# Two-layer streaming attention encoder: the probabilities of both heads turned by DMA transposes in the second layer

## The chip, the cores and the metric

The kernel runs on one core of one Trainium2 chip. The metric is the time of one execution on the device in microseconds; before the change the median of three runs is 2216.19 us (2215.74 to 2218.65).

## The reference

Two attention layers over a prompt of 2048 frames and a sample of 64 frames, model width 1024, 16 heads of 64. The change lies in the second layer's prompt attention. Cut to that:

```python
def gated_attention_layer(x_p, x_s, ck, cv, norm_g, w_in, q_g, k_g, w_out, ...):
    qp, kp, vp, gp = project(x_p, norm_g, w_in, q_g, k_g, n_heads, n_kv)   # RMS norm, one matmul, norms of q and k
    op = prompt_band_attention(qp, kp, vp, past_chunks, bias_fn, sinks)     # own chunk of 64 and 8 before it
    y_p = x_p + (op * jax.nn.silu(gp)) @ w_out
    ...

# inside, for each head and chunk (second layer: no sinks)
s = q @ k.T * dh ** -0.5 + bias
p = jax.nn.softmax(s, axis=-1)
o = p @ v
```

Inputs and outputs are float32. The kernel keeps that precision with half-precision matmuls by splitting most operands into a high part and a remainder (hi = f16(x), lo = x - hi) and adding their products.

## The kernel before, in words

The first layer (`layer_a`), its output projection, the second layer (`layer_b`) and its output projection follow each other. The order of TensorE's instructions is written out by hand: attention steps alternate with pieces of projection matmuls, the "filler". `filler.to(mark)` emits projection work up to a mark. The other engines and the DMA queue of SP are ordered by a scheduler, within the dependencies and within hints: `bg.anchor(...)` names instructions behind which later background work (the norms of queries and keys, gates, splits of weights and activations) has to stand on the same engine. Each engine runs its instructions in order.

The second layer runs over 8 head pairs, `hp` 0 to 7, and in each over 9 units: 8 of 256 prompt frames (two tiles of 128) and the sample. A unit of the prompt has four attention steps, in the order tile 0 and tile 1 of head 0, then tile 0 and tile 1 of head 1. A step (`scores(it, i, h)`) is:

- TensorE: scores of 128 queries against up to 640 keys into an `sb` buffer of PSUM (L1416, L1417). There are two `sb` buffers.
- VectorE: adds the bias and takes the minimum of the negated scores (L1420) into `p` (float32) and `nm`.
- ScalarE: exp and the sums (L1429).

The products with the values need the probabilities with keys on the partitions, so each 128x128 block is transposed. `TURNED` (L54) lists the heads that do this by DMA; it holds for head pairs 1 to 7 only (`turned(it, h)`), not for head pair 0 and not for the sample.

- A head in `TURNED`: VectorE adds log(2^14) to `nm` ahead of exp (L1425). `parts` copies `p` to f16 on ScalarE (L1463) and subtracts that from `p` on GpSimd (L1464), both into one of three slots of a tile that the profile calls `values`. One step later `turn_p` issues the DMA transpose on SP (L1472) into a `pt` tile; there are two `pt` buffers, one for each head and unit. `turned_products` (matmuls at L1561) follows `LAG` = 4 steps after the step of the second tile.
- Another head: one step later `values` transposes block by block on TensorE (L844) into a new `sb` buffer; ScalarE (L816) and VectorE (L817) split that into `ph` and `pl`. `products` (matmuls at L1600) follows three steps after the step of the second tile.

When head 1 is done, the unit's gate is transposed into an `sb` buffer and multiplied in (L1237, L1247, L1249, L1250).

The queries and keys of a unit come from `head_norm`: squares on GpSimd (L756), sums on VectorE (L757), two GpSimd steps (L760 adds a constant, L761 takes the power -1/2), scaling on VectorE (L774), then TensorE transposes into `tp` and ScalarE and VectorE split them (L1355 to L1371). The copies `q<-q` go over SP (L1360), the projections' inputs too (`xx<-xsb`, L527).

Of the kernel before, what the change touches and what calls it, by code (L numbers as in the profile page):

```python
# [50 lines left out]
HB, WB_, PB, VB = 2.0 ** 10, 2.0 ** 14, 2.0 ** 14, 16.0  # L51
LAG = 4
HALF = 5 * 2 * P
TURNED = (0,)  # L54

@with_exitstack
def hybrid_encoder_kernel(
# [47 lines left out]
    def psum(tag, cols, bufs, pool=None):  # L105
        uid[0] += 1
        return (pool or pp).tile([P, cols], F32, tag=tag, name=f"{tag}_{uid[0]}", bufs=bufs)
# [77 lines left out]
    def times(dst, a, c):  # L185
        nc.vector.tensor_scalar(dst, a, c, 1.0, op0=ALU.mult, op1=ALU.mult)
# [33 lines left out]
    def input_across(h):  # L220
# [4 lines left out]
        times(o[:, 1:2], e, 1 / (HB * WB_))  # L225
        times(o[:, 2:3], e, 0.5 / VB if h > 0 and len(TURNED) == 2 else 0.5 / (VB * PB))

# [194 lines left out]
    bg = Background()  # L422
# [833 lines left out]
    def layer_b():  # L1256
# [126 lines left out]
        def scores(it, i, h):  # L1383
# [50 lines left out]
            if turned(it, h):  # L1434
                parts(it, i, h, p, nk // P)
            if c == w - 1:
                nc.vector.reciprocal(it.sm[:n, :w], it.sm[:n, :w])
                if turned(it, 0) and len(TURNED) == 1:
                    part = it.sm[:n, TURNED[0] : w : 2]
                    nc.vector.tensor_scalar(part, part, PB, 1.0, op0=ALU.mult, op1=ALU.mult)  # L1440
# [14 lines left out]
        def turned(it, h):  # L1455
            return it.unit[0] != NU and it.hp > 0 and h in TURNED

        def parts(it, i, h, p, m):
            held["turn"] = r = (held["turn"] + 1) % 3
            it.two = it.two if i else {}  # L1460
            it.two[i] = two = held["two"][:, 5 * r : 5 * r + m]
            pv = p.rearrange("p (c q) -> p c q", q=P)[:, :m]
            hi = nc.scalar.copy(two[:, :, 0, :], pv)  # L1463
            lo = nc.gpsimd.tensor_tensor(two[:, :, 1, :], pv, two[:, :, 0, :], op=ALU.subtract)  # L1464
            bg.anchor(hi, lo)
            it.two[i] = two.rearrange("p c l q -> p (c l q)")

        def turn_p(it, i, h, two):
# [32 lines left out]
        def then(it, i, h):  # L1501
            late = it.hp > 0 and len(TURNED)
            if it.unit[0] == NU:
                return [
                    (1, "values", (it, i, h)), (2 + late, "call", lambda: sample_outputs(it)),
                    (3 + late, "call", lambda: sample_turned(it)),
                ]
            last = i == len(it.unit[2]) - 1
            if turned(it, h):
                two = it.two[i]  # L1510
                todo = [(1, "call", lambda: turn_p(it, i, h, two))]
                return todo + [(LAG, "call", lambda: turned_products(it, h))] * last
            return [(1, "values", (it, i, h))] + [(2 + late, "products", (it, h))] * last
# [55 lines left out]
        def gates(it):  # L1569
            u, T, tiles = it.unit  # L1570
            n = tiles[0][2]
            GT = psum_b("sb", 1024, 2) if it.hp and len(TURNED) else psum("tp", 512, 1)
            for e, (_, t0, _) in enumerate(tiles):
# [348 lines left out]
```

## Time and profile before

| | |
|---|---|
| median of three runs | 2216.19 us |
| the profiled execution | 2214.94 us, span 2213.1 us |
| granted TensorE clock, mean | 0.991 |
| busy share of the span | PE 95%, DVE 71%, ACT 64%, POOL 45% |
| DMA transposes (L1472) | 112, from 1055.0 to 2048.1 us, median 3.5 us from issue to landing |

PE is TensorE's matmuls, PEld its weight loads, DVE VectorE, ACT ScalarE, POOL GpSimd, SP the engine that issues the DMAs. In rows of groups, "x112 | 140.0, 1250 | 243.5" means 112 instructions, 140.0 us busy in total, 1250 ns each on average, and 243.5 us of idle time of the engine just ahead of them, with what ended it. In rows of waits the three numbers are the total in us, how many, and the longest. In rows of the timeline they are the start and the duration in us.

### The profile page before, as it was taken

Reading aid. Unit: us, or ns where it says so; the run is one execution under the profiler, and the core shown is the slowest. Engines: PE = TensorE matmul, PEld = TensorE weight load, DVE = VectorE, ACT = ScalarE, POOL = GpSimd, SP = SyncE. Lnnn points to the kernel's source line nnn. Section 1 sums busy time; section 2 is a strip of 40 time slices with the busy share of each in tenths; the row PEclk is TensorE's granted clock in tenths of the full one; section 3 lists DMA queues with packets and bytes.
Section 4 is the critical chain, followed back from the end, with each engine's and each line's share of the span. In section 5 each row is a group of like instructions: output and inputs, shape, how many; then the busy total and the mean of one; then the engine's idle time right before and its main releaser. Section 6 shows DMA issues by size and latency. Waiting matters only on the chain. (4 is left out here: it accounts for less than half of the span.)

```text
span 2213.1 us, 41369 instructions
## 1 busy us (share of the span) xinstructions
PE 2102.7 (95%) x13441; PEld 1522.1 (69%) x13441; DVE 1563.9 (71%) x4105; ACT 1425.7 (64%) x3610; POOL 1004.9 (45%) x1509
## 2 busy tenths in 40 slices
PE   7999999999999999989999999999999998998999
PEld 6887888788889997556555555555555555556888
DVE  6769777677676456778676777877767778677642
ACT  6878878777785333666666766766667667576420
POOL 5645544334454455853444444444454445443000
PEclk9999999999999999999999999999999999999999
DMA  8856546856546667545465565654756546345664
GB/s 274 275 162 215 179 127 219 234 160 195 170 129 184 210 204 244 171 143 167 107 186 133 130 177 130 173 148 121 186 133 155 159 111 172 91 104 136 199 200 124
DMA packets 383096, 372.87 MB, mean 168 GB/s; under 512 B 174672, under 2 KB 320352, under 8 KB 382848
## 3 DMA queue, kind: packets, MB, share of 16 engines
q1 hardware_dynamic: 382880, 370.23, 58.0%
q8 instruction: 106, 1.74, 0.3%
q14 instruction: 110, 0.90, 0.1%
HBM read 257.59 MB, written 73.43 MB: 150 GB/s over the span
## 5 line engine op out<-in xcount | busy, mean ns | idle before, releaser
L679 PE MATMUL pj<-wh,xx 128*128 128x512 f16 (+2 forms) x1648 | 643.4, 390 | 5.8 <-ACT pb L702 4.1
L681 PE MATMUL pj<-wh,xx 128*128 128x512 f16 (+2 forms) x1648 | 625.5, 380 | 2.5 <-POOL xx L564 2.5
L680 PE MATMUL pj<-wh,xx 128*128 128x512 f16 x1024 | 391.5, 382 | 0.0
L1429 ACT ACTIVATE p<-p,nm 128x640 f32<-128x640 f32 (+5 forms) x264 | 198.9, 753 | 213.6 <-DVE nm L1420 108.0
L1765 PE MATMUL pj<-xx,wh 128*128 128x264 f32 (+1 forms) x1024 | 290.0, 283 | 8.5 <-DVE res L1775 4.1
L1766 PE MATMUL pj<-xx,wh 128*128 128x264 f32 (+1 forms) x1024 | 287.7, 281 | 0.0
L1464 POOL TENSOR_TENSOR values<-p,values 128x640 f16<-128x640 f32 (+2 forms) x112 | 140.0, 1250 | 243.5 <-ACT values L1463 243.5
L680 PE MATMUL pj<-wl,xx 128*128 128x512 f32 (+1 forms) x624 | 233.9, 375 | 2.2 <-DVE wl L470 2.2
L564 POOL TENSOR_TENSOR xx<-xraw,xx 128x528 fp32r<-128x528 f32 (+4 forms) x144 | 184.9, 1303 | 87.8 <-ACT xx L563 74.6
L1420 DVE CUSTOM_DVE_ANT_0 p<-sb,BT 128x640 f32<-128x640 f32 (+5 forms) x272 | 195.6, 719 | 38.3 <-PE sb L1417 35.6
L1250 POOL TENSOR_TENSOR o<-gt,o 128x256 f32<-128x256 f32 (+1 forms) x132 | 101.1, 766 | 206.2 <-ACT p L1156 89.6
L761 POOL TENSOR_TENSOR f<-f,mhalf 128x4 f32<-128x4 f32 (+2 forms) x187 | 187.0, 1000 | 13.8
L681 PEld LDWEIGHTS <-xx 128*128 128x128 f16 x1024 | 100.9, 99 | 125.9 <-issue 3.9
L774 DVE TENSOR_TENSOR pa<-pa,f 128x256 f32<-128x256 f32 (+3 forms) x221 | 136.5, 618 | 55.1 <-POOL f L761 50.6
L1156 ACT ACTIVATE p<-p,nm 128x257 f32<-128x257 f32 (+2 forms) x272 | 134.3, 497 | 50.1 <-DVE nm L1150 41.7
L756 POOL TENSOR_TENSOR sq<-pa 128x256 f32<-128x256 f32 (+2 forms) x187 | 123.7, 663 | 72.5 <-ACT pa L715 38.2
L679 PEld LDWEIGHTS <-xx 128*128 128x128 f16 x1024 | 101.0, 99 | 71.5 <-issue 2.7
L680 PEld LDWEIGHTS <-xx 128*128 128x128 f16 x1024 | 100.9, 99 | 70.3 <-issue 2.9
L817 DVE SCALAR_TENSOR_TENSOR pl<-sb,ph 128x640 f16<-128x640 f32 (+4 forms) x144 | 106.2, 737 | 58.2 <-ACT ph L816 56.5
L1767 PE MATMUL pj<-xx,wl 128*128 128x264 f32 x512 | 145.0, 283 | 1.0 <-DVE wl L463 1.0
L1767 PE MATMUL pj<-xx,wh 128*128 128x264 f16 x512 | 142.1, 277 | 1.3 <-DVE wh L460 1.3
L1150 DVE CUSTOM_DVE_ANT_0 p<-sa,BT,nsink 128x256 f32<-128x256 f32 (+2 forms) x272 | 117.3, 467 | 34.6 <-PE sa L844 29.5
(273 smaller groups left out, 5290.7 us busy)
## 6 DMA issues: line engine op xcount, KB each, us to landing
xx<-xsb SPq DMA_DIRECT2D x112, 512.0 KB, 4.2
xx<-xsa SPq DMA_DIRECT2D x88, 512.0 KB, 4.8
xraw<-oga SPq DMA_DIRECT2D x64, 264.0 KB, 3.6
xraw<-ogb SPq DMA_DIRECT2D x64, 264.0 KB, 3.6
xsa<-xx SPq DMA_DIRECT2D x32, 512.0 KB, 4.0
scan<-in_w_in_b_dram SPq DMA_DIRECT2D x64, 256.0 KB, 4.6
wl<-in_w_in_b_dram SPq DMA_DIRECT2D x64, 256.0 KB, 4.0
xraw<-in_x_dram SPq DMA_DIRECT2D x40, 256.0 KB, 3.9
```

What stands on the lines that cost most here:

```text
L564: nc.gpsimd.tensor_tensor(lo, rv, wide(hi), op=ALU.subtract)
L679: nc.tensor.matmul(ps[:n, :C], xh, wh, start=k == 0, stop=False)
L680: nc.tensor.matmul(ps[:n, :C], xh, wl, start=False, stop=False)
L681: nc.tensor.matmul(ps[:n, :C], xl, wh, start=False, stop=k == KC - 1)
L761: nc.gpsimd.tensor_tensor(fv, fv, mhalf[:n, :H], op=ALU.pow)
L774: nc.vector.tensor_tensor(sv, sv, fv.unsqueeze(2).to_broadcast([n, H, HD]), op=ALU.mult)
L1420: mi = nc.vector.tensor_tensor_reduce(out=p[r, :nk], in0=S[r, o : o + nk], in1=b, op0=ALU.add, op1=ALU.min, scale=1.0, scalar=3e38, accum_ ...
L1429: ex = nc.scalar.activation(p[:n, :nk], p[:n, :nk], AF.Exp, scale=-1.0, bias=it.nm[:n, c : c + 1], accum_out=it.sm[:n, c : c + 1],)
L1464: lo = nc.gpsimd.tensor_tensor(two[:, :, 1, :], pv, two[:, :, 0, :], op=ALU.subtract)
L1765: nc.tensor.matmul(ps[:, :OT], wh, oh, start=k == 0, stop=False)
L1766: nc.tensor.matmul(ps[:, :OT], wh, ol, start=False, stop=False)
L1767: nc.tensor.matmul(ps[:, :OT], wl, oh, start=False, stop=k == KC - 1)
```

## The change

Two lines. Head 1 joins `TURNED`, so in head pairs 1 to 7 both heads take the DMA path: `parts`, `turn_p` and `turned_products` in place of `values` and `products`. And GpSimd's remainder `lo` is no longer named to `bg.anchor`, so that GpSimd's background work has no order against it. With two heads in `TURNED`, the factor 2^14 is in the sums of both, so the constant that undoes it moves: the multiplication of head 0's sums (L1440) is left out, and the gate's factor loses 1/2^14.

```diff
@@ -51,7 +51,7 @@
 HB, WB_, PB, VB = 2.0 ** 10, 2.0 ** 14, 2.0 ** 14, 16.0
 LAG = 4
 HALF = 5 * 2 * P
-TURNED = (0,)
+TURNED = (0, 1)
 
@@ -1462,7 +1462,7 @@
             pv = p.rearrange("p (c q) -> p c q", q=P)[:, :m]
             hi = nc.scalar.copy(two[:, :, 0, :], pv)
             lo = nc.gpsimd.tensor_tensor(two[:, :, 1, :], pv, two[:, :, 0, :], op=ALU.subtract)
-            bg.anchor(hi, lo)
+            bg.anchor(hi)
             it.two[i] = two.rearrange("p c l q -> p (c l q)")
```

## The prediction

> **What bounds the kernel now.** I read the engine shares and slices first, then cut the span by stage, then asked who waits in the stage that changes.
>
> ```profile
> span 2213.1 us, 41369 instructions
> PE 2102.7 (95%) x13441; PEld 1522.1 (69%) x13441; DVE 1563.9 (71%) x4105; ACT 1425.7 (64%) x3610; POOL 1004.9 (45%) x1509
> ...
> PE   7999999999999999989999999999999998998999
> ```
>
> TensorE is busy nearly everywhere. The transposed probabilities exist only in head pairs 1 to 7 of the second layer: their DMA transposes bound the stage.
>
> ```profile
> L1472 SPq DMA_TRANSPOSE pt<-values x112: 1180/1362/2389, 1055.0 to 2048.1; - x112
> ```
>
> So the stage is 1055 to 2050 us. It stands here with a stretch of the first layer:
>
> ```profile
> core 0: us, PE busy (x) PEld busy (x) DVE busy (x) ACT busy (x) POOL busy (x), PEclk, DMA share, GB/s
> 200.00:600.00 400.00, 396.33 (x2184) 320.63 (x2183) 297.63 (x876) 309.22 (x864) 178.56 (x347) 1.00 0.61 187
> 1055.00:2050.00 995.00, 937.52 (x5809) 567.72 (x5808) 741.76 (x1911) 668.09 (x1676) 466.13 (x695) 0.99 0.55 142
> ```
>
> In 995 us PE idles 57; DVE is at 75%, ACT 67%, POOL 47%. In the first layer PE stays at 99% beside a DVE at 74% and an ACT at 77%, so such loads alone don't hold PE back. What PE waits for in the changed stage:
>
> ```profile
> PE sb L844 <- DVE nm L1420: 13.6, 6, 2.3
> PE sb L1416 <- DVE nm L1420: 12.7, 10, 1.7
> PE tp L844 <- DVE pa L774: 8.0, 5, 1.7
> PE sb L844 <- DVE pl L817: 7.7, 10, 1.2
> ```
>
> Three of the four are waits for a free `sb` buffer, of which there are two; scores, PE-transposed probabilities and gates share them. So the bound is PE's own order of work, plus some 34 us in which it waits for `sb`.
>
> **What goes.** How many 128x128 blocks head 1 has is read from head 0's remainders, which have the same shapes (whole trace, by shape; head 1 equals head 0):
>
> ```profile
> L1464 POOL TENSOR_TENSOR values<-p,values 128x640 f16<-128x640 f32 x84 | 117.8, 1403 | 211.9 <-ACT values L1463 211.9
> L1464 POOL TENSOR_TENSOR values<-p,values 128x512 f16<-128x512 f32 x7 | 8.1, 1159 | 1.7 <-ACT values L1463 1.7
> L1464 POOL TENSOR_TENSOR values<-p,values 128x384 f16<-128x384 f32 x7 | 6.4, 913 | 15.7 <-ACT values L1463 15.7
> L1464 POOL TENSOR_TENSOR values<-p,values 128x256 f16<-128x256 f32 x7 | 4.7, 674 | 4.8 <-ACT values L1463 4.8
> L1464 POOL TENSOR_TENSOR values<-p,values 128x128 f16<-128x128 f32 x7 | 3.0, 428 | 9.4 <-ACT values L1463 9.4
> ```
>
> 84x5 + 7x(4+3+2+1) = 490 blocks, so 490 PE transposes go. What one costs in PE's order, from the timeline:
>
> ```profile
> 1504.62 0.38 PE L679 MATMUL pj<-wh,xx 128*128 128x512 f16 x1
> 1504.83 0.38 PE L680 MATMUL pj<-wh,xx 128*128 128x512 f16 x1
> 1505.05 0.38 PE L681 MATMUL pj<-wh,xx 128*128 128x512 f16 x1
> 1505.26 0.49 PE L844 MATMUL sb<-ident,p 128*128 128x128 f32 x3
> 1505.59 0.38 PE L679 MATMUL pj<-wh,xx 128*128 128x512 f16 x1
> ```
>
> Projection matmuls start 0.215 us apart. With three transposes between, the gap is 1505.59 - 1505.05 = 0.54, so 0.325 for three, 0.108 each; 490 x 0.108 = **53 us**. All of it lies on PE, the path. The group rows of the stage bound it from above:
>
> ```profile
> L844 PE MATMUL sb<-ident,p 128*128 128x128 f32 x501 | 75.5, 276 | 25.1 <-DVE nm L1420 13.6 <-DVE pl L817 7.7 <-ACT values L719 2.3
> L816 ACT ACTIVATE ph<-sb 128x640 f16<-128x640 f32 (+2 forms) x111 | 69.7, 628 | 19.6 <-PE sb L844 18.7
> L817 DVE SCALAR_TENSOR_TENSOR pl<-sb,ph 128x640 f16<-128x640 f32 (+2 forms) x111 | 81.8, 737 | 49.3 <-ACT ph L816 48.0
> L1463 ACT CAST values<-p 128x640 f16<-128x640 f32 (+2 forms) x111 | 73.0, 658 | 1.8
> L1464 POOL TENSOR_TENSOR values<-p,values 128x640 f16<-128x640 f32 (+2 forms) x111 | 139.6, 1258 | 241.7 <-ACT values L1463 241.7
> L1425 DVE TENSOR_SCALAR nm<-nm 128x1 f32<-128x1 f32 x111 | 16.3, 147 | 1.4
> ```
>
> 75.5 / 501 = 0.151 us of busy time each would make it 74; the busy time contains the pipeline's tail, so I take 53 and keep 74 for the range.
>
> A unit of two tiles now takes seven `sb` buffers (four scores, two transposes, one gate transpose) and will take five. Of the 13.6 + 12.7 + 7.7 = 34 us of waits I take half away, **17 us**, since the score chain itself gets no shorter; bounds 0 and 34.
>
> **What comes.** ACT: 112 copies of 658 ns for 112 casts of 628 ns, +3 us, nothing. DVE: 112 x 737 ns leave and 112 x 147 ns (the shift of the minimum) come: -66 us, off the path; 56 small multiplications of the sums leave too. POOL: 112 more subtractions, 112 x 1.25 = +140 us: from 466 in 995 to 606 in some 930, 65%. The products with the values keep their shapes; they read `pt` in place of `ph` and `pl`, in one burst, one step later.
>
> SP: 112 more transposes.
>
> ```profile
> pt<-values SPq DMA_TRANSPOSE x112, 3.5
> ...
> 1413.68 1.67 SPq L1472 DMA_TRANSPOSE pt<-values  x1
> ...
> 1422.62 1.26 PE L1561 MATMUL o<-pt,values 128*128 128x256 f16 x12
> ```
>
> The second transpose of a unit is issued at 1413.68 and lands some 3.5 us later; its products start at 1422.62, so about 5.4 us are to spare. Head 1 gets the same schedule (issue one step after its scores, products four steps after the second), two steps behind head 0, so the landing stays hidden; cover gone, a late landing costs PE its excess over that slack. Two things newly stand in line. The next unit's first transpose of a head now reuses that head's `pt` buffer (two buffers, two heads) and must wait on SP for the products at 1422.62 to end at 1423.88; behind it on SP stand the prefetches of `xx`, the copies `q<-q` and the stores. In this trace that next transpose went out at 1423.52, so this wait is tenths of a microsecond:
>
> ```profile
> 1423.52 1.43 SPq L1472 DMA_TRANSPOSE pt<-values  x1
> ```
>
> And the three slots for high and low parts come round every three steps instead of every six on average: ACT's copy, with its evacuations queued behind it, waits if the transpose of three steps before has not landed. The stage has 7 x (8 x 4 + 1) = 231 steps, 4.3 us each, so three are 13 us; a landing of 3.5 us leaves room.
>
> DMA engines: layer one's stretch moves 187 GB/s at a share of 0.61, 0.0033 for each GB/s. The 980 blocks of 32 KB (high and low) are 32 GB/s of the stage's 142; the other 110 would take 0.36, which leaves 0.19 for the transposes. Doubled, in 930 us, the share is (0.55 + 0.19) x 995 / 930 = 0.79, an estimate: dense, not full.
>
> A rule of the Trainium skill speaks against the change. The Trainium skill, "VectorE: DVE Perf Modes", The three transpose paths, puts a 128x128 bf16 transpose at 390 ns on TensorE and 1309 ns on the DMA crossbar and says to use TensorE where PSUM will do; by it 980 added blocks would be 1283 us of DMA, longer than the stage. The trace disagrees: ten blocks land in about 3.5 us.
>
> The costs that remain are POOL's. Its subtraction slows DVE beside it:
>
> ```profile
> 1499.70 1.16 POOL L1464 TENSOR_TENSOR values<-p,values 128x512 f16<-128x512 f32 x1
> 1499.76 1.38 DVE L774 TENSOR_TENSOR pa<-pa,f 128x256 f32<-128x256 f32 x1 [1.40 <-POOL f L761]
> ...
> 1504.13 0.42 DVE L774 TENSOR_TENSOR pa<-pa,f 128x256 f32<-128x256 f32 x1 [0.52 <-POOL f L761]
> ...
> L774 DVE TENSOR_TENSOR pa<-pa,f 128x256 f32<-128x256 f32 x108 | 73.0, 676 | 34.0 <-POOL f L761 32.9
> ```
>
> The same scaling took 1.38 us beside a subtraction and 0.42 alone; the mean of 676 ns means 108 x 0.256 = 28 us of such slowing now. (The Trainium skill, "GPSIMD Engine Reference", Specifications, says that GpSimd's SBUF interfaces are shared with VectorE and that DVE instructions with two SBUF inputs contend; this row agrees.) POOL's work rises by 140 / 466 = 30%; 30% of the 28 us and of the 40.0 us that L774 waits for POOL (next fence) is 20 us. Seen by PE in full: **+20 us**; if DVE's slack hides it, 0; its other end is the rival below. The dropped order hint costs no instruction: it only frees GpSimd's background steps (squares, powers) to stand ahead of a subtraction, which shortens this wait if anything; I take 0, between -12 (30% of the 40.0 us given back) and 0.
>
> **Sum.** The profiled execution took 2214.9 us (span 2213.1), the median of the runs is 2216.2, 1.3 above. 2214.9 - 53 - 17 + 20 = 2164.9, so **2166** on the median's scale. This forecast's own range: 2216 - 53 - 34 + 0 = 2129, or with 74 for the blocks 2108, against 2216 - 53 + 20 = 2183; since both good ends together are unlikely I keep 2135 to 2190.
>
> **Rivals.**
>
> *GpSimd's chain takes over (slower).* Place: squares, sum, power on POOL, scaling L774 on DVE, then PE's transposes into `tp` for the next unit's queries. POOL works in order, so each new subtraction, with its wait for ACT's copy, stands ahead of a power.
>
> ```profile
> DVE pa L774 <- POOL f L761: 40.0, 55, 1.4
> ...
> POOL values L1464 <- ACT values L1463: 241.7, 81, 15.1
> ```
>
> Price: one subtraction ahead of the last norm in each of 56 units, 56 x 1.40, and L774 slowed in each, 56 x 0.96: 132 us if PE sees all of it, 2216 - 53 + 132 = 2295. It decides from 53 / 132 = 40% on. For it: PE already waits 8.0 us for `pa`, and POOL's waits for the copy average 3 us. Against: POOL is idle half the time, most steps of the norm are two or more steps ahead of their use, and the hint that kept background work behind the subtraction is gone. At 55 to 60% it gives 2240. Chance 0.22.
>
> *The DMA side saturates (slower).* If one holds all queues from issue to landing, 224 x 3.5 = 784 us, and the other traffic's 0.36 x 995 = 358 us on top make 1142 us, 147 more than now: 2363. For: the landing time alone. Against: at that price 112 transposes and the rest would already show a share of (392 + 358) / 995 = 0.75, and it is 0.55. (The Trainium skill's rule on the three transpose paths would come out on this side.) A milder form, late landings at the ends of head pairs, where weights and scans load, costs some 2 us for each of 7 pairs and unit and ends near 2225. Chance 0.08.
>
> *The time comes back elsewhere (no change).* PE's order is shorter but evacuations and norms, at DVE 75% and ACT 67%, take up the slack: 2216 +- 4. Against: the first layer's 99%. Chance 0.06.
>
> That the change doesn't do what it says: hardly possible; in the changed code no head of these pairs calls the path with PE transposes.
>
> **How the numbers follow.** Forecast 0.64, GpSimd's chain 0.22, DMA 0.08, no change 0.06. Time 2166. The range runs from 2135 to 2240: it takes the forecast's own range, no change, and the milder slower cases; what lies outside (full exposure, saturation, both good ends at once) is under 2 in 10. A measurement of this kernel tells about 0.2%, 4.4 us, from no change. Faster by more: 0.64. Within: 0.06. Slower: 0.22 + 0.08 = 0.30.
>
> **What would show it.** Right: in the changed profile `sb<-ident,p` falls by 490; PE's busy time in the stage falls by 53 to 74 us; the waits of L1416 for `nm` shrink; POOL's L1464 stands at 224 with 280 us, and PE stays above 94% of a stage of about 945 us; the landing of `pt` stays under 5 us with nobody waiting for it. Wrong: PE's busy time falls as said but its idle time rises by as much, with PE's transposes into `tp` waiting for `pa` (GpSimd's chain), L1561 waiting for `pt` or ACT's L1463 for a slot (DMA), or a stage not shorter than 995 us.

## The result and the profile after

The changed kernel took 2266.20 us (median of four runs, 2263.46 to 2270.11), the kernel before 2216.47 (four runs): ratio 1.0228, 95% interval 1.0208 to 1.0247. The prediction was 2166, faster; the range ended at 2240. The page of the changed kernel, TensorE's row and its slices:

```profile
span 2261.7 us, 40979 instructions
...
PE 2081.2 (92%) x12951; PEld 1475.8 (65%) x12951; DVE 1518.3 (67%) x4049; ACT 1433.0 (63%) x3610; POOL 1147.0 (51%) x1621
...
PE   7999999999999998999889879799898897897999
```

The 490 transposes are gone (13441 to 12951 matmuls), VectorE is lighter and GpSimd heavier, as foretold. But TensorE's slices in the stage, 9 before with a few exceptions, are now 8 or 7 in more than half of the places. The stage now ends near 2100 us. Its whole, and one stretch at the end of a head pair (columns as in the stage table before):

```profile
1055.00:2100.00 1045.00, 916.65 (x5374) 522.40 (x5372) 700.47 (x1867) 678.46 (x1683) 609.61 (x810) 0.95 0.71 165
1457.00:1476.00 19.00, 9.83 (x47) 4.60 (x46) 11.02 (x25) 9.18 (x23) 8.11 (x12) 0.82 0.83 205
```

PE idles 128 us in the stage, where it idled 57. Its busy time on the whole page fell by 22 us only (2102.7 to 2081.2), so 71 us more of idling less these 22 make the loss of some 50. What it waits for there, longest first:

```profile
PE pj L679 <- ACT wh L467: 27.7, 12, 4.2
PE pj L680 <- DVE wh L470: 24.0, 18, 2.6
PE sb L1416 <- DVE nm L1420: 15.8, 12, 2.7
PE tp L844 <- DVE scl L213: 12.3, 5, 2.5
PE tp L197 <- DVE KB L1371: 12.0, 6, 3.8
PE o L844 <- POOL o L1526: 10.3, 6, 1.9
...
PE o L1561 <- DMA pt<-values: 0.2, 1, 0.2
```

The two longest are new: projections wait 51.7 us for weights, `wh`, that ScalarE (L467) and VectorE (L470) split for the next head pair. The transposes by DMA, in contrast, are waited for once, 0.2 us. Their landing and GpSimd's subtractions after:

```profile
DMA to landing us min/median/max: 2.3/3.8/7.6
```

```profile
L1464 POOL TENSOR_TENSOR values<-p,values 128x640 f16<-128x640 f32 (+2 forms) x224 | 286.4, 1278 | 139.9 <-ACT values L1463 138.0
```

Both are as forecast: 3.5 us became 3.8, and 112 subtractions became 224 with little change in each. The timeline of TensorE at the end of a head pair, its matmuls that waited for a split:

```profile
1459.20 0.38 PE L679 MATMUL pj<-wh,xx 128*128 128x512 f16 x1 [0.79 <-ACT wh L467]
1460.60 0.38 PE L680 MATMUL pj<-wh,xx 128*128 128x512 f16 x1 [1.02 <-DVE wh L470]
1464.64 0.38 PE L680 MATMUL pj<-wh,xx 128*128 128x512 f16 x1 [2.59 <-DVE wh L470]
1469.20 0.58 PE L679 MATMUL pj<-wh,xx 128*128 128x512 f16 x1 [3.96 <-ACT wh L467]
```

and ScalarE's splits there, with those of the same head pair in the kernel before, whose first use was at 1437.88:

```profile
1458.43 0.72 ACT L467 ACTIVATE wh<-wl,gsb 128x512 f16<-128x512 f32 x1
```

```profile
1400.49 0.71 ACT L467 ACTIVATE wh<-wl,gsb 128x512 f16<-128x512 f32 x1
1401.82 0.71 ACT L467 ACTIVATE wh<-wl,gsb 128x512 f16<-128x512 f32 x1
1406.32 1.33 ACT L467 ACTIVATE wh<-wl,gsb 128x512 f16<-128x512 f32 x2
1430.57 0.72 ACT L467 ACTIVATE wh<-wl,gsb 128x512 f16<-128x512 f32 x1
...
1437.88 0.38 PE L679 MATMUL pj<-wh,xx 128*128 128x512 f16 x1
```

Before, the first split started 37 us and the fifth 7 us ahead of the first use; the sixth started at 1433.86, and its matmul came at 1442.75. After, the sixth split ends at 1459.15, and its matmul starts at 1459.20.

The code says why. Background work (these splits among it) is emitted by `bg.share`, which is called behind each step's scores and, in `due`, once behind each `values`:

```python
for x in vals:
    values(*x, short)
    bg.share(BL, BP_, KC)
for fn in short + rests:
    fn()
```

A head that goes by DMA has no `values`. A unit had six shares (four behind scores, two behind head 1's values) and now has four, so the next weights are split when TensorE asks for them, behind whatever stands in ScalarE's and VectorE's order.

### The profile page after: what moved, and what is told of

Its sections match the earlier page's. It is cut to its first block, busy times and chain, and to the rows that moved or that the text cites. A ratio compares the mean times of both kernels' runs of the same rounds, so it can differ in the third digit from the quotient of the medians.

```text
span 2261.7 us, 40979 instructions
## 1 busy us (share of the span) xinstructions
PE 2081.2 (92%) x12951; PEld 1475.8 (65%) x12951; DVE 1518.3 (67%) x4049; ACT 1433.0 (63%) x3610; POOL 1147.0 (51%) x1621
## 5 line engine op out<-in xcount | busy, mean ns | idle before, releaser
L679 PE MATMUL pj<-wh,xx 128*128 128x512 f16 (+2 forms) x1648 | 649.9, 394 | 32.3 <-ACT wh L467 27.7
L680 PE MATMUL pj<-wh,xx 128*128 128x512 f16 x1024 | 397.8, 388 | 24.0 <-DVE wh L470 24.0
L1464 POOL TENSOR_TENSOR values<-p,values 128x640 f16<-128x640 f32 (+2 forms) x224 | 286.4, 1278 | 139.9 <-ACT values L1463 138.0
L680 PE MATMUL pj<-wl,xx 128*128 128x512 f32 (+1 forms) x624 | 234.2, 375 | 2.6 <-DVE wl L470 2.6
L774 DVE TENSOR_TENSOR pa<-pa,f 128x256 f32<-128x256 f32 (+3 forms) x221 | 144.5, 654 | 56.5 <-POOL f L761 51.2
L680 PEld LDWEIGHTS <-xx 128*128 128x128 f16 x1024 | 102.0, 100 | 113.0 <-issue 39.4
L756 POOL TENSOR_TENSOR sq<-pa 128x256 f32<-128x256 f32 (+2 forms) x187 | 116.8, 625 | 106.2 <-ACT pa L715 72.6
L679 PEld LDWEIGHTS <-xx 128*128 128x128 f16 x1024 | 102.5, 100 | 85.1 <-issue 9.2
L1463 ACT CAST values<-p 128x640 f16<-128x640 f32 (+2 forms) x224 | 146.9, 656 | 5.3
```

What stands on the lines that cost most here:

```text
L679: nc.tensor.matmul(ps[:n, :C], xh, wh, start=k == 0, stop=False)
L680: nc.tensor.matmul(ps[:n, :C], xh, wl, start=False, stop=False)
```

## The experiments

Four theories: **A**, the missing shares; **B**, GpSimd's added subtractions; **C**, the DMA side; **D**, the dropped hint (`lo` no longer named to `bg.anchor`). Differences of about 10 us are not put down to a cause here: any edit lets the scheduler reorder the four engines, and e9_pool_small, which only adds work, came out 9 us faster. Times are medians. The kernel before was timed again beside each group of runs: 2218.8 beside e1 to e4, 2218.8 beside e5 to e8, 2219.0 beside e9 to e12.

**e1_shares.** The changed kernel, the shares put back.

```diff
-                todo = [(1, "call", lambda: turn_p(it, i, h, two))]
+                todo = [(1, "call", lambda: (turn_p(it, i, h, two), h and bg.share(BL, BP_, KC)))]
```

> The changed kernel, with one background share (bg.share) added behind each of head 1's DMA transposes, where the PE-transposed path had one behind its values. Theory A (the background work, above all the splits of the next head pair's weights, is drained only by shares, and head 1 lost its two of six in each unit, so that TensorE waits for late splits): the waits of L679 and L680 for wh (51.7 us in the changed kernel) fall under 10 us and the time comes down by 40 to 100 us, to 2165 to 2225. Theory B (GpSimd's subtractions delay the norms) and theory C (the DMA engines are too dense): 2255 to 2275, as the changed kernel.

2217.2 us, ratio to before 0.9995 (0.9982 to 1.0007): 49 us come back. Its waits in the stage:

```profile
PE pj L680 <- DVE wh L470: 6.1, 6, 1.0
...
PE pj L679 <- ACT wh L467: 2.1, 6, 0.5
```

8.2 us in place of 51.7. Theory A holds, but the run ends level with before, not 50 us under it: something else takes the rest. TensorE also waits here for the copies `q<-q`, which the kernel before never made it do:

```profile
PE sb L1416 <- DMA q<-q: 10.6, 5, 2.5
```

On SP these copies stand right behind a transpose: around the wait that ends at 1467.14, the transpose is issued at 1463.34 and takes 1.34 us, and the first copy follows at 1464.77. The same wait is 12.4 us in e7_rest_on_vector and 8.1 in e10_more_shares; no run takes it away by itself.

**e4_fewer_shares.** The converse: the kernel before loses the two shares and nothing else.

```diff
                     values(*x, short)
-                    bg.share(BL, BP_, KC)
+                    if x[0].hp == 0 or x[0].unit[0] == NU:
+                        bg.share(BL, BP_, KC)
```

> The kernel before (head 1 still transposed on TensorE) without the background share behind head 1's values in head pairs 1 to 7, so four shares a unit in place of six. Theory A: TensorE waits 30 us or more for wh at L679 and L680 and the time rises by 30 to 60 us, to 2245 to 2276. Theories B and C: 2216 within 8 us, since neither GpSimd's nor the DMA's load changes.

2242.1 us, 1.0116 (1.0089 to 1.0144): 23 us slower, a little under what A expected, with the same waits, absent before (18.8 us, where A expected 30 or more):

```profile
PE pj L679 <- ACT wh L467: 14.0, 6, 2.3
...
PE pj L680 <- DVE wh L470: 4.8, 11, 1.0
```

So losing the shares costs time without any second head on DMA, and costs twice as much with it.

**e2_hint_kept and e3_hint_only.** Each half of the change alone. The first edit is against the changed kernel; the second run is the kernel before with the opposite edit.

```diff
-            bg.anchor(hi)
+            bg.anchor(hi, lo)
```

> The changed kernel with GpSimd's order hint put back (both heads turned by DMA, remainder still named to the anchor). Theory D (the dropped hint is the loss): back to 2216 or at least 20 us under 2266. Theories A, B and C: within 10 us of 2266.

> The kernel before with the hint left out alone. Theory D: slower by 20 us or more. Theories A, B and C: 2216 within 6 us.

With both heads turned and the hint kept 2260.7 us, 1.0188 (1.0167 to 1.0209); the interval touches that of the changed kernel. The hint left out of the kernel before: 2204.9 us, 0.9939 (0.9924 to 0.9953), 14 us faster, which no theory expected. Theory D is out: the hint's half of the change is a gain by itself; beside a second turned head none was seen. In e3 L774, the scaling of queries and keys on VectorE, met a GpSimd subtraction less often: by the timelines 16 of 109 overlap one, where 31 of 108 did before, and it takes 493 ns on average in the stage in place of 653 (all shapes). In e2 the longest wait of TensorE is the one that the prediction's first rival named:

```profile
PE tp L844 <- DVE pa L774: 34.8, 15, 5.4
```

It was 8.0 us before and is gone in the changed kernel. So with two heads turned the rival's chain does hold TensorE up as long as the hint is kept; the time is nearly the same without it.

**e5_pool_load.** The kernel before with GpSimd's added load alone.

```diff
                 parts(it, i, h, p, nk // P)
+            elif turned(it, 0):
+                junk = t("junk", [P, 640], 1, F16)
+                nc.gpsimd.tensor_tensor(junk[:, :nk], p[:, :nk], p[:, :nk], op=ALU.subtract)
```

> The kernel before, with one more GpSimd subtraction of the same size in each of head 1's steps of head pairs 1 to 7 (p - p into a tile that nobody reads); the rest is unchanged. It prices GpSimd's 140 us of added work by itself. Theory B (this load, through order on GpSimd and through VectorE beside it, is what eats the 53 us of TensorE work that the change saves): 15 to 55 us slower than before, 2232 to 2272. Without B: within 6 us of before.

2271.8 us, 1.0251 (1.0226 to 1.0275): 53 us slower, at the top of B's range. GpSimd's other work did not grow; VectorE's did. Its rows in the stage, by shape (line numbers from L1430 on stand three higher in this run):

```profile
L774 DVE TENSOR_TENSOR pa<-pa,f 128x256 f32<-128x256 f32 x110 | 115.0, 1045 | 33.7 <-POOL f L761 32.3
...
L1443 DVE TENSOR_SCALAR sm<-sm 128x2 f32<-128x2 f32 x55 | 28.7, 522 | 1.2
```

L774 went from 676 to 1045 ns: 83 of its 110 now overlap a subtraction and take 1.21 us, the others 0.53. TensorE then waited for `sb` until VectorE had read it:

```profile
PE sb L844 <- DVE pl L817: 32.0, 32, 2.4
PE sb L844 <- DVE nm L1420: 21.4, 7, 3.2
```

**e9_pool_small.** The same place, but GpSimd's added instruction is a power of 128x4 elements.

```diff
+            elif turned(it, 0):
+                junk = t("junk", [P, 4], 1)
+                nc.gpsimd.tensor_tensor(junk, small, p[:, :4], op=ALU.pow)
```

> The kernel before with one more GpSimd power of 128x4 elements in each of head 1's steps in head pairs 1 to 7, behind the same exp as e5_pool_load's subtraction. It takes 1.0 us in the place of 1.25, but reads almost nothing from SBUF. Theory B1 (the loss of e5_pool_load, 53 us, is queueing in GpSimd's order): some four fifths of it, 30 to 50 us slower than before, 2247 to 2270. Theory B2 (it is VectorE's instructions with two inputs in SBUF that run slowly beside a GpSimd subtraction): under 12 us slower, and L774 stays near 676 ns.

2209.7 us, 0.9963 (0.9949 to 0.9978), not slower. GpSimd was occupied nearly as long, 113.8 us where e5's added subtractions took 125.0:

```profile
L1438 POOL TENSOR_TENSOR junk<-small,p 128x4 f32<-128x4 f32 x111 | 113.8, 1025 | 45.3 <-ACT p L1429 45.1
```

while L774 stayed at 654 ns; the 60 of them that overlap a power take 0.42 us on average. So the price of e5 is not GpSimd's queue. It is VectorE's instructions running slowly beside large GpSimd subtractions; whether reading or writing does it was not tested.

**e6_dma_load.** The kernel before, each of its transposes issued a second time.

```diff
+        def turn_again(two):
+            m = min(two.shape[1], 8 * P)
+            junk = t("junk", [P, 8 * P], 1, F16)
+            nc.sync.dma_start_transpose(junk[:, :m].rearrange("p (c q) -> p c q", q=P), two[:, :m])
...
-                todo = [(1, "call", lambda: turn_p(it, i, h, two))]
+                todo = [(1, "call", lambda: turn_p(it, i, h, two)), (2, "call", lambda: turn_again(two))]
```

> The kernel before, with each of head 0's 112 DMA transposes issued a second time one step later into a tile that nobody reads (8 of the 10 blocks at most, for lack of room): some 80 to 85% of the DMA work and all of the SP issues that the change adds. Theory C (the DMA side eats the saving): 15 to 55 us slower than before, with TensorE waiting for q<-q, wh or xx. Without C: within 6 us of before.

2228.3 us, 1.0055 (1.0036 to 1.0075): between the two expectations. The added load alone costs some 10 us, a difference of the size that is not put down to a cause here, and none of the waits that C named grew in it. Nobody reads the second transposes, so the run says nothing on late landings or on SP's wait for a free `pt`.

**e8_half_transposes.** e1 with head 1's transposes moving half the blocks.

```diff
+            if h:
+                flat = two.rearrange("p c l q -> p (c l q)")
+                ...
+                it.two[i] = flat[:, : m * P]
+                return
```

> The kernel of e1_shares, with head 1's DMA transposes moving the high parts alone (half of the blocks; the remainder is still subtracted on GpSimd but not used, the products take the high part twice, so the output leaves the remainder out). As many transposes, half of the added DMA bytes. Theory C: 10 us or more under e1_shares, 2180 to 2207. Theory B: within 6 us of 2217.

Head 1's high parts are counted twice in this kernel and its remainders are left out, so it serves for its time alone. 2215.5 us, 0.9977 (0.9961 to 0.9994), against 0.9995 for e1: a quarter less transpose work in all changes next to nothing. Theory C, as the load of the DMA engines, is out as the main cause. The waits for `q<-q` stay at 8.8 us, and as many transposes are issued as in e1.

**e7_rest_on_vector.** e1 with head 1's remainder on VectorE.

```diff
-            lo = nc.gpsimd.tensor_tensor(two[:, :, 1, :], pv, two[:, :, 0, :], op=ALU.subtract)
+            lo = (nc.gpsimd, nc.vector)[h].tensor_tensor(two[:, :, 1, :], pv, two[:, :, 0, :], op=ALU.subtract)
```

> The kernel of e1_shares with head 1's remainder subtracted on VectorE in place of GpSimd, so that GpSimd has the load of before; VectorE has lost 66 us to the change and gets some 90 back. Theory B: 10 us or more under e1_shares (2217), 2180 to 2207. Theory C: as e1_shares within 6 us, or slower since VectorE is the fuller engine.

2192.2 us, 0.9888 (0.9867 to 0.9909): 25 us under e1. VectorE took 87 us of subtractions on and yet its gates (L783) and weight splits (L470) got faster. In e1 and then here, in the stage:

```profile
L783 DVE SCALAR_TENSOR_TENSOR pb<-sq,pb 128x128 f32<-128x128 f32 (+1 forms) x116 | 77.9, 672 | 31.1 <-ACT sq L782 30.5
L470 DVE SCALAR_TENSOR_TENSOR wh<-wl,gsb,wh 128x512 f16<-128x512 f32 x48 | 49.2, 1035 | 4.1 <-ACT wh L467 4.1
```

```profile
L783 DVE SCALAR_TENSOR_TENSOR pb<-sq,pb 128x128 f32<-128x128 f32 (+1 forms) x116 | 46.8, 404 | 25.0 <-ACT sq L782 23.6
L470 DVE SCALAR_TENSOR_TENSOR wh<-wl,gsb,wh 128x512 f16<-128x512 f32 x48 | 40.8, 868 | 0.0
```

L774 hardly moved (752 to 725 ns for the shape 128x256). The move also makes the subtraction itself shorter (776 ns on VectorE, 1260 for those still on GpSimd) and takes it out of GpSimd's order, so that the 25 us are VectorE's shorter durations is argued from these rows, e5 and e9, and not shown alone. This is the first of these pages on which a time under the kernel before goes with the removed TensorE work:

```profile
PE 2057.2 (94%) x12951; PEld 1470.1 (67%) x12951; DVE 1558.5 (71%) x4161; ACT 1434.8 (66%) x3610; POOL 1027.3 (47%) x1509
```

**e11_vector_no_shares.** e7's edit without the shares.

> The changed kernel with head 1's remainder on VectorE alone, without the added shares: the fourth corner beside the changed kernel (2266), e1_shares (2217) and e7_rest_on_vector (2192). If the two causes add, 2266 - 25 = 2241 (2234 to 2248). If they feed each other (late splits are late because GpSimd is), nearer to 2215; if the shares are all, 2255 or more.

2228.4 us, 1.0042 (1.0027 to 1.0057). The four corners: changed 2266, shares 2217, remainder moved 2228, both 2192. Alone they give 49 and 38, together 74: they overlap by 13, so 2228 lies between the case in which they add and the one in which they feed each other. The waits for `wh` are back (21.5 us at L679, 15.3 at L680).

**e10_more_shares.** e7 with a share behind the transposes of both heads, eight a unit.

```diff
-lambda: (turn_p(it, i, h, two), h and bg.share(BL, BP_, KC))
+lambda: (turn_p(it, i, h, two), bg.share(BL, BP_, KC))
```

> The kernel of e7_rest_on_vector with a background share behind the transposes of both heads, so eight a unit in place of six. Theory A: the last waits for wh (6.6 us) go and the time falls by 3 to 15 us, to 2177 to 2189. If six are enough: within 4 us of 2192, or slower, since background work then stands ahead of the steps' own.

2183.2 us, 0.9844 (0.9814 to 0.9875), the fastest of all: 36 us under the kernel before, 83 under the changed one. It is 9 us under e7, as A expected, but by the measure above so small a difference alone doesn't show the cause. L470 takes 757 ns, and no wait for `wh` is among TensorE's six longest.

**e12_one_head_vector.** e3 with head 0's remainder on VectorE; head 1 still on TensorE.

```diff
-            lo = nc.gpsimd.tensor_tensor(two[:, :, 1, :], pv, two[:, :, 0, :], op=ALU.subtract)
+            lo = nc.vector.tensor_tensor(two[:, :, 1, :], pv, two[:, :, 0, :], op=ALU.subtract)
```

> The kernel of e3_hint_only (one head by DMA, hint left out) with head 0's remainder on VectorE: GpSimd loses 140 us, VectorE gets some 90. Theory B: if GpSimd's load costs what e5_pool_load showed, also below the load of before, 15 to 50 us under e3_hint_only (2205): 2155 to 2190. If the price starts only above the load of before, or VectorE at 75% is full: 2200 to 2225.

2225.9 us, 1.0031 (1.0015 to 1.0048), 21 us slower than e3 and just above both expectations, though L774 fell to 452 ns. VectorE's share of the stage rose from 73% to 76%; which wait makes the loss was not settled. Moving a subtraction to VectorE paid where the second head's splits (L817) had left that engine (e1 to e7), and not where they were still on it.

## Why the prediction was wrong, point by point

- *490 transposes, 53 us:* the count is right, and the size where TensorE isn't made to wait. From the kernel before to e7 PE's busy time falls by 46 us, and between e3 and e7, both without the hint, by 58 (2114.9 to 2057.2). In the changed kernel it fell by 22, so the prediction's own sign of being right, 53 to 74 us, did not show there. The granted clock in the stage is 0.95 in place of 0.99; how much of the rest that explains was not worked out.
- *17 us of waits for `sb`:* right in amount, in part by luck. The waits of L844 went from 21.3 to 1.2 us, but those of L1416, which were to shrink, rose from 12.7 to 15.8.
- *Landings hidden:* right. Landing took 3.8 us at the median, 0.2 us were waited for. The wait of SP for a free `pt` was mis-sized: 50.5 us over 37 transposes, 1.4 us each, not tenths. In the changed kernel TensorE waited for the copies queued behind for 0.8 us only; with the shares back it is 10.6 (e1).
- *DMA share 0.79, "dense, not full":* right. The measured 0.71 over 1045 us would be 0.80 over 930. The milder DMA rival ended at 2225, 59 us over the forecast, to which its 2 us for each head pair don't add up; e6's added load cost 10. VectorE's waits for the `scan` loads (L175) rose from 17.9 + 3.6 to 26.5 + 17.9 us, but they are 26.0 + 13.4 in e3, which adds no transpose.
- *GpSimd's 20 us:* too small without the shares (38 us, the changed kernel to e11), about right with them (25, e1 to e7; both with 87 us of subtractions added to VectorE), and wrong in place. The 20 us were L774's, in its length and its wait for the power. From e1 to e7 it is L783 and L470 that get shorter, by 31 and 8 us in all. The rival expected TensorE's transposes into `tp` to wait for `pa`; that wait (8.0 us before) is not on the list after.
- *The hint at 0, between -12 and 0:* alone it gave 14 us, the sign right and the size just outside. With both heads turned, leaving it out came out 5 us slower (e2 to the changed kernel), with intervals that touch.
- **The step that failed** is the part-by-part list itself. "One burst, one step later" was taken to be all that changes in the order of the work, and ScalarE's and VectorE's parts were priced by their durations alone ("+3 us, nothing" and "off the path"). Leaving `values` also left out the share behind it, so a unit has four calls for background work in place of six, and TensorE waits 51.7 us for late weight splits, a term that the sum doesn't have. No row of the profile before could show this wait; the loop in `due` does. It cost 49 us (e1), all of the 50 us that were forecast as the gain; the second cause, GpSimd beside VectorE, was in the sum with 20 us where it cost 25 to 38.
- *"The first layer's 99%"* was used to show that such loads don't hold PE back, and against the rival that the time comes back elsewhere. It said nothing here: the first layer's loop calls its own shares (L1215, L1219), which the change leaves as they were.

From the changed kernel to the forecast are 100 us: 49 for the shares, 25 for GpSimd beside VectorE once these are back, and 9 more with eight shares reach 2183. The last 17 us were not taken apart. The forecast also allowed 20 us for the load on GpSimd which these runs move away, so what is open is rather more than 17.

Two things that the list leaves out belong there. Three waits of TensorE come about once in each head pair: L844 for the scale factors (`scl` L213), L197 for L1371, and L844 for the sample's product (L1526). The kernel before had only these:

```profile
PE tp L197 <- DVE KB L1371: 4.0, 1, 4.0
PE tp L844 <- DVE scl L213: 1.3, 5, 0.3
```

Together they are 5.3 us before, 34.6 in the changed kernel, 38.2 in e1, 21.2 in e7 and 10.6 in e10, and at most 11.3 in the runs that add one load to the kernel before or take only its shares (e4, e5, e6). No run takes them apart. Nor does any test by itself what else changes with `TURNED`: `then` adds `len(TURNED)` to the steps after which the sample's outputs follow, so they come one step later.

## What to carry to other kernels

When an instruction path is replaced, look at what else its call site did: in a hand-paced kernel, calls that emit background work ride on the paths, and their count per unit is part of the schedule. A load moved to an engine with idle time isn't free if it slows another engine's instructions; price it by a run that adds that load alone. And a change made of two edits is worth splitting first: here one half, alone, was a gain of 0.6%.

## What the runs showed of the hardware

L774 on VectorE, with two inputs in SBUF, took 0.42 us alone. In the kernel before, the 31 of 108 that overlap a large GpSimd subtraction take 1.21 us, the others 0.46, 676 ns on average; in e5 83 of 110 overlap one, and the average is 1045. It isn't the number of subtractions that counts but how often the two meet: the changed kernel has twice the subtractions of before, and L774 takes 712. Powers of 128x4, nearly as long on GpSimd, left it at 654 (e9). A small VectorE instruction with one SBUF tensor input (the sums' scaling, 128x2) slowed too, from 178 ns before (L1440) to 522 in e5. TensorE's granted clock is lower where it stalls: in the stretch from 1457 to 1476 us, where PE idles half the time, it is 0.82, and after 3.96 us of waiting the same matmul took 0.58 us in place of 0.38. (The Trainium skill, "TensorE: Matmul & The Clock Gate", Why this matters for your kernels, advises against idle gaps over about 3 us between bursts; this row agrees.)
